# A hybrid decoder layer on one core: w_down and the first gate/up sets with tokens in place

## The chip, the cores and the metric

The kernel runs on one core of a Trainium2 chip. The metric is the device time of one execution in microseconds; lower is better. The median of 3 runs of the kernel before is 2718.86 us, the lowest 2718.18, the highest 2719.04.

## The reference

One layer on 512 tokens of width 2048, all in float32: two token mixers side by side (latent attention and a gated delta rule), then a SwiGLU block. The change touches the end of it:

```
x = x + gt_a * mix
h = rmsnorm(x, norm_ffn) * (1 + sc_f) + sh_f          # (512, 2048)
gate, up = split(h @ w_gate_up)                        # w_gate_up (2048, 2 * 5632)
x = x + gt_f * ((silu(gate) * up) @ w_down)            # w_down    (5632, 2048)
return rmsnorm(x, final_norm)
```

`gt_f` is one vector of 2048 values, from the conditioning vector c.

## The kernel before

**Precision.** Each float32 operand is split into a rounded high half and a rest (`hi`, `lo`; ACT casts, DVE subtracts), and each product is three matmuls into one PSUM bank: high by high, high by low, low by high. In a matmul one operand of 128 x 128 stays in the array (it is loaded by PEld), and the other streams past it, 256 or 512 columns wide. A name like `m<-xh,hi` lists the streaming operand first and the one in place second.

**The order of the work.** Python code makes *units* (`Unit`: load, split, mms, pre, post). `Driver` keeps some units loaded and two split ahead of the one whose matmuls run, and steps side chains between matmuls. All instructions are recorded under one line (`L477`), and `Score` then sets the order on DVE and ACT by a planner: it has a price for each operation (`durations`), a latest start for each (`latest`), and a model of the run (`order`). PE, POOL and SP keep the order of the code. Tiles come from pools: 68 slots of 512 columns, 5 `raws`, 4 `his`, 4 `los`, 8 PSUM banks.

**The SwiGLU block.** `w_gate_up` is worked in 11 sets of 512 gate and 512 up channels (the first two of 256 each). The sets 2 to 11 (`big`) use Strassen's seven products over halves of the tokens and of the inner dimension: 16 units of two sums of weights, their splits and 24 or 18 matmuls of 512 columns, with the tokens in place. Eight PSUM banks hold four products of two token blocks for the first 8 units; three more products are added to them in the other 8. One sum of weights is written to DRAM (`s_dram`) in the first half and read back in the second. The result is turned back to channels by rows with short runs of transposes (`aT`), and kept in DRAM (`f_dram`).

The first two sets are plain. `gu0` runs twice over its weights, once for each half of the tokens, since the second half becomes ready later; `gu_both` works on both halves at once. Both keep the weights in place and stream 256 tokens at a time.

**w_down.** Its 44 blocks of 128 rows are worked as 4 (`dn(36, n)`), 16 in seven-product parts (`strassen_down(0, n)`, n = 0 to 3, 512 channels each), 4 (`dn(40, n)`), 16 in seven-product parts (`strassen_down(1, n)`) and 4 last rows (`last_dn`). A seven-product part has 8 units of 42 matmuls; the weights are in place and 256 tokens stream. Each result is scaled by `gt_ffn` and added in DRAM to `x2_dram`, which holds the residual x, channels by rows: POOL issues a transfer that adds.

**The end.** The residual comes back from `x2_dram` (`back`). For the first 256 tokens `last_unit` keeps the weights in place (`dnl`, 256 columns), and that half of the output leaves channels by rows. For the other 256 the residual is turned (`x2T`, two runs of 16 transposes, copied out by ACT to `x2t`), and `token_unit` keeps the tokens in place (`dnt`, 512 columns); each unit ends with a product with the gate row, a sum, a square with its row sum on ACT, and a product with the row of `final_norm`. After the last unit of a token block, `token_rstd` takes the root in three steps and `scaled` writes the block out. The host puts the two halves together.

Of the kernel before, what the change touches and what calls it, by code (L numbers as in the profile page):

```python
# [144 lines left out]
class Op:  # L145
# [20 lines left out]
    def durations(self):  # L166
# [6 lines left out]
        if self.pe:  # L173
            if self.name == "transpose":
                return 45 + 0.345 * n, 280.0
            if any(a.rounded for a in self.reads):
                return n / 2.4 + 13.5, n / 2.4 + 176.5
            t = 222.0 if n <= 1 else 17.0 if n <= 32 else 116.0 if n <= 64 else n / 0.6 + 9
            return t, t + 165
        if self.engine == "vector":  # L180
            if self.name in ("tensor_tensor", "tensor_copy"):
                d = 148 + 1.05 * n
            elif self.name == "tensor_reduce":
                d = 148 + 1.05 * m
            elif self.name == "reciprocal":
# [96 lines left out]
class Score:  # L282
# [67 lines left out]
    def latest(self):  # L350
# [17 lines left out]
        for _ in range(self.ROUNDS):  # L368
            out, after = [0.0] * n, {}
            for k in range(n - 1, -1, -1):  # L370
                op = ops[k]
                seen = self.LANDING + op.move if op.dma else op.seen
                v = min([out[j] - seen for j in self.users[k] + late[k]], default=end - seen)
                if op.pe:
# [10 lines left out]
    def order(self):  # L385
# [33 lines left out]
        for _ in range(n):  # L419
# [67 lines left out]
def block_kernel(ctx: ExitStack, tc: tile.TileContext, a: dict, out, out_t):  # L487
# [248 lines left out]

    w_in = a["w_in"][0]
# [216 lines left out]
    n_out = C("n_out", [P, 16])  # L954

    def load_scalars():
        load(n_out[:], a["out_norm"])
# [761 lines left out]
    s_ffn, sh_ffn, gt_mix, gt_ffn, gt_neg, gt_mneg = (C(n, [P, 16]) for n in ("s_ffn", "sh_ffn", "gt_mix", "gt_ffn", "gt_neg", "gt_mneg"))  # L1719
# [565 lines left out]
    def strassen_down(ks, n):  # L2285

        def outputs(res):
            for h in range(2):
                for f in range(2):
                    t = res.pop("gp"[f] + str(h))  # L2290
                    for j in range(2):
                        k = 4 * n + 2 * f + j
                        nc.scalar.activation(half_of(t, k), half_of(t, k), AF.Copy, scale=(gt_neg if f else gt_ffn)[:, k:k + 1])
                    nc.gpsimd.dma_start(x2_dram[h, 2 * n + f], t[:], accum_op=ALU.add)
                    yield

        def freed(k):
            if n == 3 and k % 2:
                down[ks][k // 2] = None
                gone[1 + ks] += 1  # L2300

        w = w_dn[2048 * ks:2048 * ks + 2048, :].rearrange("(h k p) n -> k p h n", h=2, p=P)
        return strassen(lambda k: w[k], 512 * n + 256, 512 * n,
                        [(c, i, j, lambda k, c=c: half_k(down[ks][k // 2][c], k)) for c, i, j in PRODUCTS],
                        lambda k: down_ready(ks, k // 2), outputs, freed, still=n == 3)
# [145 lines left out]
    def gu_done(s, ps):  # L2451

        f = {}

        def done(j, h):
            if h == 0:
                return
            for h in range(2):
                fs, v = slice(256 * (j % 2), 256 * (j % 2) + 256), ps[j][:, 256 * h:256 * h + 256]
                if j < 2:  # L2460
                    if j == 0:
                        f[h] = S("sl")
                    nc.scalar.activation(f[h][:, fs], v, AF.Silu)
                else:
                    nc.vector.tensor_tensor(f[h][:, fs], f[h][:, fs], v, ALU.mult)
                if j == 3:
                    side(f_dram[s, h], f[h][:])
        return done

    def gu_both(s):  # L2470

        st = {}

        def unit(k0):
# [8 lines left out]
            def pre():  # L2483
                if k0 == 0:
                    st["ps"] = [PS(f"gu{s}") for _ in range(4)]
                    st["done"] = gu_done(s, st["ps"])

            def after(j, h):
                st["done"](j, h)

            mms = []
            for kk in range(2):
                k = k0 + kk
                for j in range(4):
                    for h in range(2):
                        for n, (wi, xi) in enumerate(((0, 0), (0, 1), (1, 0))):
                            mms.append(lambda kk=kk, k=k, j=j, h=h, n=n, wi=wi, xi=xi: mm(
                                st["ps"][j][:, 256 * h:256 * h + 256], box["w"][wi][:, kk, tok(j)], half_k(h2T[h][k // 2], k)[xi],
                                start=k == 0 and h == 0 and n == 0, stop=k == KT - 1 and n == 2, skip_group_check=True))
                        if k == KT - 1:  # L2500
                            mms[-1] = lambda m=mms[-1], j=j, h=h: (m(), after(j, h))

            def post():
                if k0 + 2 == KT:
                    for q in range(4):
                        h2T[1][q] = None

            return Unit(start, split, mms, pre, post, late=k0 + 2 == KT)
# [3 lines left out]
    def dn_done(n, k0):  # L2512
        def done(ps):
            for j in range(4):
                k = 4 * n + j
                t = S("y")
                nc.scalar.activation(t[:], ps[j][:], AF.Copy, scale=gt_ffn[:, k:k + 1])
                nc.gpsimd.dma_start(x2_dram[:, k // 2, :, 256 * (k % 2):256 * (k % 2) + 256].rearrange("h p n -> p h n"),
                                    t[:].rearrange("p (h n) -> p h n", h=2), accum_op=ALU.add)
# [8 lines left out]
    def ffn():  # L2528
        def gu0():
            us, st = [], {}  # L2530

            def done(ps):
                done_ = gu_done(0, ps)
                for j in range(4):
                    for h in range(2):
                        done_(j, h)

            for h in range(2):
                half = fm_set("gu0", gu_loads(0), 512, KT, lambda k, h=h: half_k(h2T[h][k // 2], k), done if h else None, st=st,
                              cols=slice(256 * h, 256 * h + 256), alone=True)  # L2540
# [5 lines left out]
                us.append(half)  # L2546
# [6 lines left out]
            with_pre(us[0], start)  # L2553
            return us[0] + us[1]
# [6 lines left out]
        def dn(k1, n):  # L2561
            return fm_set(f"dn{k1}_{n}", lambda k0, nk: plain(w_dn, k1 + k0, nk, 512 * n, 512), 512, 4,
                          lambda k: (aT[k1 + k][0][:], aT[k1 + k][1][:]), dn_done(n, k1), late=True)

        LAST = 32
        wl = {}

        def last_weights(n, k0):
# [6 lines left out]
            def split():  # L2575
                raw = box.pop("raw")
                for kk in range(2):
                    wl[n, k0 + kk] = hilo(raw[:, kk, :], "wl")
# [3 lines left out]
        def last_dn():  # L2582

            weights = [last_weights(n, k0) for n in range(4) for k0 in (0, 2)]
            for k, u in enumerate(strassen_down(1, 3)):
                if k == 1:
                    def start():
                        chains["back"] = drv.add(back())
                    with_pre([u], start)
                yield u  # L2590
                for _ in range((0, 0, 0, 0, 0, 0, 1, 1)[k]):
                    yield weights.pop(0)
            for q in range(8):
                u = last_unit(FIRST, [2 * q, 2 * q + 1])
                if q == 0:
                    with_pre([u], lambda: drv.finish(chains["act"]))
                with_pre([u], lambda q=q: back_to(q))
                yield u
                for _ in range(min(2, len(weights))):
                    yield weights.pop(0)  # L2600
            yield act(load_rows)
            yield Unit(pre=lambda: back_to(15), mms=[lambda t=t, n=n: turned(t, n) for t in range(2) for n in range(4)])
            sf = C("sf", [P, 2, 6])
            for t in range(2):
                for n in range(4):
                    for cs in (slice(0, 256), slice(256, 512)) if (t, n) == (1, 3) else (slice(0, 512),):
                        yield token_unit(t, n, sf[:, t, :], cs)

        back_n = [0]

        def back():

            yield from until(lambda: gone[2] >= 1)
            for i in (2, 3):
                reload_a(LAST + i)
                yield
            yield from until(lambda: gone[2] >= 2)
            for h in range(2):
                for q in range(8):
                    if q == 6 and h == 0:  # L2620
# [222 lines left out]
```

## Time and profile before

| | |
|---|---|
| median of 3 runs | 2718.86 us |
| profiled execution | 2718.32 us |
| its span, first to last instruction | 2716.5 us |
| TensorE busy | 2698.4 us, 15304 matmuls |
| VectorE busy | 2130.9 us |
| ScalarE busy | 1213.8 us |
| DMA traffic | 562 MB, 207 GB/s on average |
| mean granted TensorE clock | 0.998 |

PE is TensorE's matmul, PEld its weight load, DVE VectorE, ACT ScalarE, POOL GpSimd, SP SyncE (here it issues loads). Lines of the profile name the output, then the inputs, without buffer numbers. The chain of waits is followed back from the last instruction; it gives the work that nothing else could have been late for.

### The profile page before, as it was taken

Reading aid. Unit: us, or ns where it says so; the run is one execution under the profiler, and the core shown is the slowest. Engines: PE = TensorE matmul, PEld = TensorE weight load, DVE = VectorE, ACT = ScalarE, POOL = GpSimd, SP = SyncE. Lnnn points to the kernel's source line nnn. Section 1 sums busy time; section 2 is a strip of 40 time slices with the busy share of each in tenths; the row PEclk is TensorE's granted clock in tenths of the full one; section 3 lists DMA queues with packets and bytes.
Section 4 is the critical chain, followed back from the end, with each engine's and each line's share of the span. In section 5 each row is a group of like instructions: output and inputs, shape, how many; then the busy total and the mean of one; then the engine's idle time right before and its main releaser. Section 6 shows DMA issues by size and latency. Waiting matters only on the chain.

```text
span 2716.5 us, 41153 instructions
## 1 busy us (share of the span) xinstructions
PE 2698.4 (99%) x15304; PEld 2349.9 (87%) x15304; DVE 2130.9 (78%) x3361; ACT 1213.8 (45%) x1717; POOL 257.7 (9%) x361
## 2 busy tenths in 40 slices
PE   9999999999999999999999999999999999999998
PEld 7888788888888888889999888888888888998997
DVE  8985666776988887688797777778787887878877
ACT  4343432442345343335573444444444446446445
POOL 0000011102001000000000000000000103013113
PEclk9999999999999999999999999999999999999999
DMA  9995555645666889524864566665655669479565
GB/s 352 353 360 195 163 168 170 201 132 178 183 185 210 314 299 325 200 86 125 268 198 143 186 202 202 205 211 200 209 193 192 221 205 224 122 192 209 142 181 173
DMA packets 315490, 562.21 MB, mean 207 GB/s; under 512 B 40772, under 2 KB 120916, under 8 KB 315288
## 3 DMA queue, kind: packets, MB, share of 16 engines
q1 hardware_dynamic: 264776, 458.99, 52.0%
q0 software_dynamic: 31872, 74.76, 10.9%
q10 hardware_dynamic: 18640, 25.83, 2.7%
q8 instruction: 120, 1.97, 0.3%
q14 instruction: 82, 0.67, 0.1%
HBM read 476.62 MB, written 83.89 MB: 206 GB/s over the span
## 4 chain that ended last, share of the span: by engine, by line
PE 99%; issue 0%; DVE 0%; DMA 0%; SPq 0%; ACT 0%; POOLq 0%; DVEq 0%
PE m L477 44%; PE gb L477 6%; PE v L477 4%; PE gu L477 3%; PE z L477 3%; PE ya L477 3%; PE ga L477 3%; PE k L477 3%; PE s L477 3%; PE dn L477 3%; PE q L477 3%; PE yb L477 3%; PE wo L477 2%; PE qk L477 2%; PE cq L477 2%; PE ckv L477 2%
## 5 line engine op out<-in xcount | busy, mean ns | idle before, releaser
L477 ACT CAST hi<-raws 128x1024 fp32r<-128x1024 f32 (+2 forms) x328 | 292.0, 890 | 419.0 <-PE m L477 251.9
L477 ACT CAST hi<-raw 128x1024 fp32r<-128x1024 f32 (+1 forms) x251 | 260.4, 1038 | 473.0 <-DMA raw<-in_w_in_dram 81.5
L477 DVE TENSOR_TENSOR lo<-raws,hi 128x1024 fp32r<-128x1024 f32 (+2 forms) x328 | 332.4, 1022 | 139.8 <-ACT hi L477 137.0
L477 DVE TENSOR_TENSOR lo<-raw,hi 128x1024 fp32r<-128x1024 f32 (+1 forms) x251 | 303.7, 1211 | 166.5 <-ACT hi L477 163.7
L477 PE MATMUL m<-xh,lo 128*128 128x256 f32 x1088 | 307.9, 283 | 0.0
L477 PE MATMUL m<-xl,hi 128*128 128x256 f32 x1088 | 307.9, 283 | 0.0
L477 PE MATMUL m<-xh,hi 128*128 128x256 f32 x1088 | 307.9, 283 | 0.0
L477 ACT CAST hi<-sums 128x1024 fp32r<-128x1024 f32 x168 | 176.4, 1050 | 231.3 <-PE m L477 191.3
L477 DVE TENSOR_TENSOR lo<-sums,hi 128x1024 fp32r<-128x1024 f32 x168 | 205.5, 1223 | 90.4 <-ACT hi L477 88.7
L477 DVE CUSTOM_DVE_ANT_0 rawm<-rawm,cbc 128x1024 f32<-128x1024 f32 x192 | 232.2, 1225 | 19.7 <-DMA rawm<-in_w_mod_dram 19.1
L477 PEld LDWEIGHTS m<-xl,hi 128*128 128x128 f32 x1088 | 208.9, 192 | 0.1
L477 PEld LDWEIGHTS m<-xh,hi 128*128 128x128 f32 x1088 | 208.9, 192 | 0.1
L477 PEld LDWEIGHTS m<-xh,lo 128*128 128x128 f32 x1088 | 208.9, 192 | 0.0
L477 PE MATMUL m<-hi,h2h 128*128 128x512 f32 x480 | 189.9, 396 | 0.0
L477 PE MATMUL m<-hi,h2l 128*128 128x512 f32 x480 | 187.2, 390 | 0.0
L477 PE MATMUL m<-lo,h2h 128*128 128x512 f32 x480 | 187.1, 390 | 0.0
L477 PEld LDWEIGHTS m<-hi,h2l 128*128 128x128 f32 x480 | 90.1, 188 | 18.9
L477 PEld LDWEIGHTS m<-lo,h2h 128*128 128x128 f32 x480 | 90.2, 188 | 17.7
L477 PEld LDWEIGHTS m<-hi,h2h 128*128 128x128 f32 x480 | 90.2, 188 | 17.6
L477 PE MATMUL gb<-hh,hi 128*128 128x512 f32 x256 | 102.0, 398 | 0.0
L477 PE MATMUL gb<-hl,hi 128*128 128x512 f32 x256 | 99.9, 390 | 0.0
L477 PE MATMUL gb<-hh,lo 128*128 128x512 f32 x256 | 99.9, 390 | 0.0
(543 smaller groups left out, 7017.1 us busy)
## 6 DMA issues: line engine op xcount, KB each, us to landing
raws<-in_w_gate_up_dram SPq DMA_DIRECT2D x400, 256.0 KB, 3.7
rawm<-in_w_mod_dram SPq DMA_DIRECT2D x192, 512.0 KB, 5.4
raw<-in_w_in_dram SPq DMA_DIRECT2D x143, 512.0 KB, 4.7
raws<-in_w_down_dram SPq DMA_DIRECT2D x128, 256.0 KB, 3.7
s_dram<-raws POOLq DMA_DIRECT2D x80, 256.0 KB, 3.2
raws<-s_dram SPq DMA_DIRECT2D x80, 256.0 KB, 2.9
rawa<-in_w_in_dram SPq DMA_DIRECT2D x32, 512.0 KB, 4.4
raws<-in_w_o_dram SPq DMA_DIRECT2D x48, 256.0 KB, 2.9
```

What stands on the lines that cost most here:

```text
L477: self.tc.keep_in_program_order(op.call(*op.args, **op.kwargs))
```

## The change

Five things change; the planner's prices change with them.

- *Seven-product parts.* `strassen_down` is replaced by `tokens_down`, the plan of `big` with w_down's weights: tokens in place, 1024 channels a part, 16 units, so 4 parts instead of 8. Weight sums go over `s_dram` and back.
- *Where results are added.* They are now tokens by rows and not scaled; they are added in a new array `down_dram`, `dn(36)` writes it first. The two results of the part before the last stay in SBUF (`kept`), and the last part's go straight into the sums read back.
- *Gate/up's first two sets* (`gu_tokens`) keep the tokens in place and stream 256 gate and 256 up channels together, 512 columns.
- *The last rows.* All 512 tokens are worked with tokens in place. w_down's last rows are multiplied by the gate row before the split. For each block of 128 tokens and 512 channels, x2 is turned straight into the PSUM bank (`turned`), and the 12 products add to it. `finished` adds the sum read back.
- *The end.* One output, tokens by rows. `token_root` needs two DVE instructions a step instead of three, and the last block's last two pieces get root and `final_norm` in one.
- *The planner's prices* for float32 matmuls, memsets, table loads, early transfers and stores.

The core of the diff:

```diff
-            t = 222.0 if n <= 1 else 17.0 if n <= 32 else 116.0 if n <= 64 else n / 0.6 + 9
+            t = 222.0 if n <= 1 else 17.0 if n <= 32 else 116.0 if n <= 64 else max(222.0, n / 1.2 + 29)
...
-                start += 1290.0
+                start = max(start, at[op.engine] + 1290.0)
...
-                done[k] = bus + 640.0 + self.SPARE
+                done[k] = bus + 640.0 + self.SPARE + (1000.0 if 800.0 < start < 6000.0 else 0.0)
...
+    def token_root(ss, inv):
+        v, y, u = (C(nm("rs"), [P, 1]) for _ in range(3))
+        nc.vector.tensor_scalar(v[:], ss, 0.5 * inv, 0.5 * EPS, op0=ALU.mult, op1=ALU.add)
...
+        for _ in range(3):
+            nc.vector.scalar_tensor_tensor(u[:], y[:], v[:, 0:1], y[:], op0=ALU.mult, op1=ALU.mult)
+            nc.vector.scalar_tensor_tensor(y[:], u[:], -1.5, y[:], op0=ALU.add, op1=ALU.mult)
+        return y
...
-    def strassen_down(ks, n):
...
+    def tokens_down(ks, n):
...
+        FIRST4 = [("m1", 0, 1, "m1", part("m1")), ("m6", 0, 0, "m6", part("m6")), ("m7", 1, 0, "m7", part("m7")),
+                  ("m5", 1, 1, "m5", part("m5"))]
+        LAST3 = [("m2", 1, 0, "m1", part("m2")), ("m4", 0, 0, "m7", part("m4")), ("m3", 0, 1, "m5", part("m3"))]
...
+            for c, w, j, bank, x in products:
+                for t in range(2):
+                    for m, (xi, wi) in enumerate(((0, 0), (0, 1), (1, 0))):
+                        def one(c=c, w=w, j=j, bank=bank, x=x, t=t, m=m, xi=xi, wi=wi):
+                            mm(ps[bank][t][:], x(q)[xi][:, 256 * kk + P * t:256 * kk + P * t + P], box["w"][w][wi][:, j, :],
...
+    def add_down(t, n, src, **kw):
+        nc.gpsimd.dma_start(down_dram[t][:, 512 * n:512 * n + 512], src, accum_op=ALU.add)
...
+    def gu_tokens(s, hts):
...
-                                st["ps"][j][:, 256 * h:256 * h + 256], box["w"][wi][:, kk, tok(j)], half_k(h2T[h][k // 2], k)[xi],
+                mm(banks[h, t][:], half_k(h2T[h][k // 2], k)[xi][:, tok(t)], box["w"][wi][:, kk, :],
...
+        def turned(t, n, ps, cs):
...
+                mm(ps[:, P * j - cs.start:P * j - cs.start + P], half_of(x2[h][k // 2], k)[:, tok(t % 2)], ident, is_transpose=True,
+                   start=P * j == cs.start, stop=False, skip_group_check=True)
...
+        def finished(t, n, ps, cs=slice(0, 512)):
+            xt, w, c = s_t[t, n][:, cs], cs.stop - cs.start, n + (cs.start > 0)
+            tmp = S("sq")
+            nc.vector.tensor_tensor(xt, xt, ps[:, 0:w], ALU.add)
+            nc.scalar.activation(tmp[:, 0:w], xt, AF.Square, accum_out=sf[:, t, c:c + 1])
+            if (t, n // 2) != (3, 1):
+                nc.vector.tensor_tensor(xt, xt, rows[4 + n][:, cs], ALU.mult)
...
+                nc.vector.tensor_tensor(raw[:], raw[:], rows[n][:].unsqueeze(1).broadcast_to([P, 2, 512]), ALU.mult)
+                hi, lo = halves(raw, 512, 2)
...
+            def at(i):
+                if i == 2:
+                    back_s(0)
+                elif i == 3:
+                    with_kept(0)
+                    back_s(1)
+                elif i == 4:
+                    with_kept(1)
+                    load_rows(g_dram)
...
+                elif i == 15:
+                    load_rows(a["final_norm"])
```

`back_s` reads four blocks of `down_dram` back into tiles `sd`, `with_kept` adds the kept results, `at(i)` runs ahead of unit i of the last part. In the two programs the matmuls of 512 columns go from 8463 to 10287, those of 256 from 5147 to 1498, and those of 128 from 732 to 780.

On PE, where w_down's last seven-product part ends and its last rows begin (`m`: a product's bank, `dnl` and `dnt`: a bank of the last rows, `x`: the residual, `kc`: the identity), before:

```order
L477 MATMUL m_4260_4400<-xh_4234,hi_4446 128x256
L477 MATMUL m_4260_4400<-xl_4235,hi_4446 128x256
L477 MATMUL m_4260_4400<-xh_4234,lo_4447 128x256
L477 MATMUL dnl_4471<-ah_4297,wlh_4438 128x256
L477 MATMUL dnl_4471<-al_4298,wlh_4438 128x256
L477 MATMUL dnl_4471<-ah_4297,wll_4439 128x256
```

and now:

```order
L482 MATMUL m_4213_4353<-hi_4478,xh_4264 128x512
L482 MATMUL m_4213_4353<-lo_4479,xh_4264 128x512
L482 MATMUL m_4213_4353<-hi_4478,xl_4265 128x512
L482 MATMUL dnt_4490<-kc,x_4277_4417 128x128 x2
L482 MATMUL dnt_4490<-kc,x_4278_4418 128x128 x2
L482 MATMUL dnt_4490<-hi_4484,ah_4453 128x512
L482 MATMUL dnt_4490<-lo_4485,ah_4453 128x512
```

The operands have changed places, the columns have doubled, and four transposes stand ahead of the products of the bank.

On SP, the loads of the last part, where before only weights stood (`raws_4393<-in_w_down_dram 128x2x256` and the like), now (`sd`: a block of the sums so far):

```order
L482 DMA sd_4368<-down_dram 128x512
L482 DMA sd_4369<-down_dram 128x512
L482 DMA sd_4370<-down_dram 128x512
L482 DMA sd_4371<-down_dram 128x512
L482 DMA raws_4377<-in_w_down_dram 128x512
L482 DMA raws_4378<-in_w_down_dram 128x512
L482 DMA raws_4377<-in_w_down_dram 128x512
L482 DMA sd_4379<-down_dram 128x512
```

The weights of a unit wait in the queue behind four blocks that are read back.

On DVE, the end of the program (`rs`: the root's steps, `xo` and `sd`: pieces of the output, `hbc`: the root of the channel-major half), before:

```order
L477 SCALAR_TENSOR_TENSOR rs_4577<-rs_4577,rs_4575 128x1
L477 TENSOR_TENSOR xo_4550<-x2t_4515,row_4513 128x512
L477 TENSOR_TENSOR xo_4556<-x2t_4516,row_4514 128x512
L477 TENSOR_TENSOR xo_4565<-x2t_4517,row_4513 128x512
L477 TENSOR_TENSOR xo_4568<-x2t_4518,row_4514 128x512
L477 SCALAR_TENSOR_TENSOR rs_4576<-rs_4577,rs_4576 128x1
L477 TENSOR_TENSOR xo_4571<-x2t_4518,row_4514 128x256 x2
L477 TENSOR_SCALAR xo_4562<-xo_4562,rs_4576 128x512
L477 TENSOR_TENSOR x_4344_4484<-x_4344_4484,hbc_4549 128x512
```

and now:

```order
L482 SCALAR_TENSOR_TENSOR rs_4556<-rs_4555,rs_4554 128x1
L482 SCALAR_TENSOR_TENSOR rs_4555<-rs_4556,rs_4555 128x1
L482 SCALAR_TENSOR_TENSOR rs_4556<-rs_4555,rs_4554 128x1
L482 SCALAR_TENSOR_TENSOR rs_4555<-rs_4556,rs_4555 128x1
L482 SCALAR_TENSOR_TENSOR sd_4410<-sd_4410,rs_4555,row_4488 128x512
L482 SCALAR_TENSOR_TENSOR sd_4430<-sd_4430,rs_4555,row_4489 128x512
```

Nothing stands between the root's steps any more, and two products follow them instead of ten instructions.

More of the change, by code (lines that the diff above doesn't have):

```diff
@@ L368, in latest @@
         for _ in range(self.ROUNDS):
-            out, after = [0.0] * n, {}
+            out, after, store = [0.0] * n, {}, end
             for k in range(n - 1, -1, -1):
@@ L2449, in gu_loads, with gu_read @@
                                (lambda r: r[:, :, 256:512], wrows(w_gu, k0, nk, DFF + 256 * s, 256))]
[L2451 to L2472, printed above, removed]
+    first_tiles = {}
+    def gu_read(s, ht, bank):
+        if s == 0:
+            first_tiles[ht] = S("g0")
+        o, g = first_tiles[ht][:, 256 * s:256 * s + 256], S("sl")
+        nc.scalar.activation(g[:, 0:256], bank[:, 0:256], AF.Silu)
+        nc.vector.tensor_tensor(o, g[:, 0:256], bank[:, 256:512], ALU.mult)
+    def gu_tokens(s, hts):
+        banks = {}
         def unit(k0):
@@ L2513, in done @@
         def done(ps):
[L2514 to L2519, printed above, removed]
+            for t in range(NT):
+                y = S("y")
+                nc.scalar.copy(y[:], ps[t][:])
+                if k0 == 36:
+                    side(down_dram[t][:, 512 * n:512 * n + 512], y[:])
+                else:
+                    add_down(t, n, y[:])
             plain_sets[0] += 1
@@ new lines, in ffn, with load_rows, back_x, back_s @@
+        sf = C("sf", [P, NT, 6])
+        def load_rows(src):
+            for i in range(4):
+                r = S("row")
+                load(r[:], src[512 * i:512 * i + 512].partition_broadcast(P))
+                rows.append(r)
+        def back_x(n):
+            for h in range(2):
+                for q in (2 * n, 2 * n + 1):
+                    x2[h][q] = S("x2")
+                    side(x2[h][q][:], x2_dram[h, q])
+        def back_s(n):
+            for t in range(NT):
+                s_t[t, n] = S("sd")
+                load(s_t[t, n][:], down_dram[t][:, 512 * n:512 * n + 512])
@@ new lines, in with_kept, with gated @@
+        def with_kept(n):
+            for t in range(NT):
+                h, j = divmod(t, 2)
+                nc.vector.tensor_tensor(s_t[t, n][:], s_t[t, n][:], kept.pop((h, j, n)), ALU.add)
+        def gated(n):
+            for t in range(NT):
+                s_ = s_t[t, n][:]
+                nc.vector.tensor_tensor(s_, s_, rows[n][:], ALU.mult)
+        def turned(t, n, ps, cs):
+            h = t // 2
+            for j in range(cs.start // P, cs.stop // P):
+                k = 4 * n + j
+                mm(ps[:, P * j - cs.start:P * j - cs.start + P], half_of(x2[h][k // 2], k)[:, tok(t % 2)], ident, is_transpose=True,
+                   start=P * j == cs.start, stop=False, skip_group_check=True)
+            if t % 2 and cs.stop == 512:
+                x2[h][2 * n] = x2[h][2 * n + 1] = None
@@ L2576, in split @@
                 raw = box.pop("raw")
+                nc.vector.tensor_tensor(raw[:], raw[:], rows[n][:].unsqueeze(1).broadcast_to([P, 2, 512]), ALU.mult)
+                hi, lo = halves(raw, 512, 2)
                 for kk in range(2):
-                    wl[n, k0 + kk] = hilo(raw[:, kk, :], "wl")
+                    wl[n, k0 + kk] = hi[:, kk, :], lo[:, kk, :]
             return Unit(start, split)
-        def last_dn():
[L2584 to L2589, printed above, removed]
-                yield u
[L2591 to L2620, printed above, removed]
-                        yield from until(lambda: gone[2] == 4 and chains["act"] not in drv.chains)
-                    x2[h][q] = S("x2")
-                    side(x2[h][q][:], x2_dram[h, q])
-                    back_n[0] += 1
-                    yield
@@ L2627, in back_to @@
-        def back_to(n):
-            while back_n[0] <= n:
-                drv.step(chains["back"])
-        FIRST = HALF[:1]
-        rows, x2t = [], []
-        def load_rows():
-            for src in (g_dram, a["final_norm"]):
-                for i in range(2):
-                    raw = raws.tile([P, 2, 512], F32, tag="raw", name=nm("row"))
-                    load(raw[:].rearrange("p j n -> p (j n)"), src[1024 * i:1024 * i + 1024].partition_broadcast(P))
-                    rows.append(raw)
-            for i in range(4):
-                x2t.append(his.tile([P, 2, 512], F32R, tag="hi", name=nm("x2t"))[:].bitcast(F32))
@@ L2745, in ffn @@
         yield from gu0()
-        yield from with_pre(gu_both(1), lambda: xc.append(drv.add(combine())))
+        both = gu_tokens(1, [(h, t) for h in range(2) for t in range(2)])
+        yield from with_pre(both, lambda: xc.append(drv.add(combine())))
         side(g_dram.rearrange("(k p) -> p k", p=P), gt_ffn[:])
-        nc.vector.tensor_scalar(gt_neg[:], gt_ffn[:], -1.0, None, op0=ALU.mult)
         for s in range(1, 11):
@@ L2773, in ffn @@
                 yield with_pre([u], more)[0]
[L2774 to L2778 removed]
+        yield from tokens_down(1, 0)
         yield from last_dn()
```

389 lines of the change are left out of this document (240 added, 149 removed).

## The prediction

> **What bounds the kernel now.** I read the page's busy times, then the chain of waits, then busy time by stage, then single stretches in order of time.
>
> ```profile
> span 2716.5 us, 41153 instructions
> PE 2698.4 (99%) x15304; PEld 2349.9 (87%) x15304; DVE 2130.9 (78%) x3361; ACT 1213.8 (45%) x1717; POOL 257.7 (9%) x361
> ```
>
> TensorE is busy for all but 18 us. That alone does not make it the bound, since a matmul's end is modelled. The chain does; its columns are start, length, what, and how many instructions.
>
> ```profile
> 1386.42 76.31 PE gu L477 x636
> 1604.70 63.96 PE m L477 x282
> 2286.81 161.27 PE m L477 x1344
> 2491.63 161.27 PE m L477 x1344
> 2652.90 23.06 PE dnl L477 x192
> 2706.06 6.47 issue
> ```
>
> Within these pieces one matmul follows another without a gap, so length over count is the price of one: 161.27 / 1344 = 120.0 ns with 256 columns (gu agrees: 76.31 / 636), and 63.96 / 282 = 226.8 ns with 512. Two of 256 cost 240.0 ns. One of 512, the same arithmetic, costs 13.2 ns less. The groups by shape give the widths.
>
> ```profile
> L477 PE MATMUL m<-xh,hi 128*128 128x256 f32 x1088 | 307.9, 283 | 0.0
> L477 PE MATMUL m<-hi,h2h 128*128 128x512 f32 x480 | 189.9, 396 | 0.0
> L477 PE MATMUL gu<-h2h,hi 128*128 128x256 f32 x256 | 72.7, 284 | 0.0
> ```
>
> The mean (283, 396) is the life of one and overlaps its neighbours'; it is not the spacing. The last column, idle before, is zero. By stage (columns: stretch, length, busy of PE, PEld, DVE, ACT, POOL with counts, granted clock, DMA share, GB/s):
>
> ```profile
> 0.00:100.00 100.00, 95.48 (x411) 77.05 (x412) 85.56 (x163) 45.83 (x61) 3.50 (x11) 1.00 0.97 352
> 1369.10:1415.40 46.30, 46.30 (x387) 46.24 (x386) 42.60 (x77) 37.55 (x58) 0.00 (x0) 1.00 0.59 183
> 1604.70:1682.75 78.05, 78.05 (x353) 64.63 (x353) 61.67 (x71) 35.07 (x43) 6.47 (x12) 1.00 0.62 203
> 2286.80:2448.10 161.30, 161.30 (x1346) 161.30 (x1345) 136.22 (x195) 81.11 (x111) 19.45 (x25) 1.00 0.62 164
> 2448.10:2491.60 43.50, 43.50 (x194) 35.99 (x194) 32.39 (x47) 27.90 (x44) 18.30 (x18) 1.00 1.04 220
> 2703.30:2716.50 13.20, 0.00 (x0) 0.00 (x0) 8.09 (x26) 3.48 (x8) 1.45 (x2) 0.68 0.51 186
> ```
>
> So TensorE's instruction stream sets the time, at a granted clock of 1.00, and a tail of 13.2 us follows it. An edit is worth what it takes from that stream or from the tail, less any new wait.
>
> **The change, part by part.** Counts are from the two programs, prices from the rows.
>
> *w_down's seven-product parts.* Before: 8 parts of 336 matmuls of 256 columns, the two 161.27 us pieces, 322.5 us. After: 4 parts of 336 matmuls of 512 columns, each 336 x 0.2268 = 76.2 us, together 304.8. **-17.7 us.** That the new stream can run at 226.8 ns is shown: the gate/up sets already run this very plan (16 units, two sums spilled to DRAM and read back, eight banks held), 78.05 us a set including 16 turns, with PE busy all the time and DVE at 61.67.
>
> *Gate/up's first two sets.* 768 matmuls of 256 (three groups of 256) become 384 of 512: 92.2 - 87.1, **-5.1 us.** The weights still have to be split on DVE, 42.60 us of work in the first set's 46.30; PE will now need about 43.7. Cover is nearly gone; see the stall term.
>
> *The last rows.* 192 dnl matmuls of 256 (23.06 us) become 96 of 512 (21.8): **-1.3 us.** The other half of these rows has 512 columns before and after.
>
> *The turns.* x2 was turned in two runs, 32 transposes; now 64, in 17 short runs each ahead of products in the same bank. Prices: the first pair of rows is a run of four between products, the second pair the old runs from first transpose to first product.
>
> ```profile
> 1673.05 0.60 PE L477 MATMUL aT<-kc,g 128*128 128x128 f32 x4
> 1673.71 0.39 PE L477 MATMUL m<-lo,h2h 128*128 128x512 f32 x1
> 2675.78 1.91 PE L477 MATMUL x2T<-kc,x 128*128 128x128 f32 x16
> 2680.59 0.48 PE L477 MATMUL dnt<-wlh,ah 128*128 128x512 f32 x1
> ```
>
> From 1673.05 to 1673.71 stand four transposes and one product: 0.66 - 0.23 = 0.44 us a run, the slower first product included. 17 x 0.44 = 7.5, less 4.8 (2675.78 to 2680.59, with eight tiny sums in it): **+2.7 us.** The gate/up tiles made with tokens in place need 16 more turns, 4 x 0.44: **+1.8 us.** The copies of turned x2 out of PSUM go; they were ACT's and hidden.
>
> *The tail.* Before, DVE has other work between its last steps.
>
> ```profile
> 2703.30 0.42 DVE L477 TENSOR_TENSOR dn<-dnt,row 128x256 f32<-128x256 f32 x1
> 2704.22 0.42 ACT L477 ACTIVATE dn<-x2t 128x256 f32<-128x256 f32 x1
> 2704.76 0.16 DVE L477 TENSOR_REDUCE sf<-sf 128x1 f32<-128x5 f32 x1
> 2705.52 0.35 DVE L477 SCALAR_TENSOR_TENSOR rs<-rs,rs 128x1 f32<-128x1 f32 x2
> 2705.91 0.16 DVE L477 TENSOR_TENSOR rs<-rs 128x1 f32<-128x1 f32 x1
> 2706.76 2.49 DVE L477 TENSOR_TENSOR xo<-x2t,row 128x512 f32<-128x512 f32 x4
> 2712.56 0.72 POOL L477 DMA_DIRECT2D out_dram<-x  x1 [6.50 <-issue]
> ```
>
> Four row products (2.49), and after them the scaling of the channel-major half, stand in the old tail; the new order has neither. New tail from PE's end: add 0.46, square to reduce 0.54, reduce and two scalar steps 0.6, six root steps at 0.195 (two in 0.39) 1.2, two products of 512 at most 1.5 beside ACT's two: 4.3 us to the last issue. From the last issue (2712.56) to the span's end are 3.9. 8.2 instead of 13.2: **-5.0 us**, between -3 (one more 2.5 us group slips in) and -6.
>
> *The start.* The planner's new costs let ACT make the first tokens' high half ahead of a cast.
>
> ```profile
> 9.57 0.83 ACT L477 CAST hi<-raw 128x768 fp32r<-128x768 f32 x1
> 10.31 0.72 ACT L477 ACTIVATE hh<-xT,s_mix 128x512 fp32r<-128x512 f32 x1
> ```
>
> That is 0.74 us earlier at best, nothing if the next loads bind; **-0.4 us.** Reordered small steps further on lie under a full TensorE: zero, and as much as a few tenths each if a wait came in.
>
> *New stalls.* None is in the trace, so bounds. Last part (336 products, 76.2 us): DVE gets 31 instructions of 1024 columns and 54 of 512; last rows (some 51 us of PE): 13 and 42, and 36 tiny ones.
>
> ```profile
> L477 DVE TENSOR_TENSOR lo<-raws,hi 128x1024 fp32r<-128x1024 f32 x160 | 195.9, 1224 | 114.8 <-ACT hi L477 112.6
> L477 DVE TENSOR_TENSOR euvw<-euvw,m 128x512 f32<-128x512 f32 x113 | 73.6, 684 | 1.3
> ```
>
> 31 x 1.224 + 54 x 0.684 = 74.9, and 15.9 + 28.7 + 36 x 0.16 = 50.4; together 125 of PE's 127 us. Back to back they are cheaper (four of 512 in 2.49, 0.62 each), so about 115 in truth. From nothing to 8.8 us (125 at the 92% that DVE reached, 42.60 / 46.30, is 136). I take **+2.5**, most of it here and some 0.5 in gate/up's first set, nearer to nothing, because that 92% was reached without a wait on PE.
>
> Sum: -17.7 - 5.1 - 1.3 + 2.7 + 1.8 - 5.0 - 0.4 + 2.5 = -22.5 us. The profiled execution took 2718.32 (span 2716.5 and 1.8 around it), 0.5 under the median of 2718.86; from the median, 2696.4.
>
> One rule speaks against the main term. The Trainium skill ("TensorE: Matmul & The Clock Gate", Back-to-back issue gap) spaces warm matmuls at N / 2.4 + 2.5 ns, so a halved count would save 2.6 ns a pair, an estimate of 4.7 us for 1824 pairs, and the sum would be about -3. The rows have 120.0 and 226.8, some 13 ns above N / 2.4 at both widths, and the measurement decides.
>
> **The rivals.**
>
> *DVE becomes the bound at the end.* For: 125 of 127 us by its durations; it has new sums with kept parts, gate products and row products there. Against: the overlap just told, and up to two units of products, some 10 us, lie split ahead. At 92% it is 2696.4 + 8.8 - 2.5 = 2703; at the 84% of the old w_down stretch (136.22 / 161.30) 125 becomes 149, 22 over, 2716. By the cheaper price (115 of 127) it costs time once DVE cannot hold 90%.
>
> *Slower: transfers bind the last part.* There 72 blocks of 256 KB stand on SP's queue (the sums so far, rows and weights) and 30 on POOL's: 26.7 MB in 76.2 us, 351 GB/s. DMA then paces sums, splits and products.
>
> ```profile
> raws<-in_w_down_dram SPq DMA_DIRECT2D x128, 256.0 KB, 3.7
> x_dram<-y POOLq DMA_DIRECT2D x32, 256.0 KB, 7.7
> 11.87 87.26 PE s L477 x383
> ```
>
> For: in the stage with added transfers the engines were full (1.04) at 220 GB/s. At that rate the part takes 121 us, 45 over; 10 are swallowed by the units ahead: 2696.4 - 2.5 + 35 = 2729. Against: that stage's x_dram transfers add in DRAM and land in 7.7 us; none of the 102 does, and plain loads ran at 352 GB/s in the first 100 us, while from 11.87 on PE took 383 products at 228 ns. It is slower than before where the rate falls below 26.7 MB / (76.2 + 10 + 25) = 240 GB/s.
>
> *The count doesn't matter.* If the 256-column products are slow for their stage's sake (PEld is busy for 161.30 of 161.30 there) and the new ones meet the same limit, they come at 2 x 120.0 = 240 ns, and the three first terms, 24.1 us, are lost: 2720.5. Against: PEld has a rest wherever 512 columns run (64.63 of 78.05), and 226.8 ns holds there. The rule of the Trainium skill's TensorE page above would end near this one, at an estimate of 2716.
>
> **How the numbers follow.** Forecast 0.77 (its own range 2693 to 2702: stall 0 to 6 and tail -6 to -3 move it by -3.5 to +5.5), DVE 0.14, transfers 0.06, count 0.03. What a measurement can tell from no change is 0.2%, 5.4 us. Faster: 0.77 and nearly all of DVE, 0.89. Same: the count and DVE's far end, 0.05. Slower: 0.06. The range leaves out transfers, count and DVE's upper part: 2690.5 (another 2 us for the start and a cheaper pace of the turns) to 2708.
>
> **What would show it.** Right: pieces of 336 products of 512 columns in the chain at 76 us, no idle PE in the w_down stretch, last product to end near 8 us, DVE over 90% in the last 127 us with PE idle under 4. Wrong: spacing above 0.23, PE idle behind lo (DVE) or behind DMA in the last part, a tail above 10 us.

## The result, and the profile after

The changed kernel takes 2733.3 us (median of 4; 2731.6 to 2734.2) against 2718.95: a ratio of 1.0053, 95% interval 1.0035 to 1.0070. It was forecast at 2696.4 and is slower than before. The profiled execution took 2731.62, span 2729.8, 13.3 more than before's 2716.5.

The page's first part, the two costliest groups of the w_down products and the group of weight sums:

```profile
span 2729.8 us, 37437 instructions
PE 2695.4 (99%) x13518; PEld 2263.3 (83%) x13518; DVE 2124.8 (78%) x3257; ACT 1181.6 (43%) x1648; POOL 230.1 (8%) x363
...
L482 PE MATMUL m<-lo,xh 128*128 128x512 f32 x448 | 178.6, 399 | 9.2 <-DVE lo L482 8.9
L482 PE MATMUL m<-hi,xh 128*128 128x512 f32 x448 | 177.6, 396 | 9.3 <-ACT hi L482 9.3
L482 DVE TENSOR_TENSOR sums<-raws,raws 128x1024 f32<-128x1024 f32 x112 | 136.5, 1219 | 26.2 <-DMA s_dram<-raws 23.8
```

"99% busy" now hides waits: before, the last column was 0.0 for the products; here it has 9.2 and 9.3 us, in front of w_down's products, and DVE's sums waited 23.8 us for stores of `s_dram` to land. The chain of waits is no longer one of matmuls (its longest pieces from 2500 us on):

```profile
2496.16 8.11 issue
2506.44 8.70 DMA s_dram<-raws
2538.68 64.01 PE m L482 x281
2602.87 8.21 DMA raws<-in_w_down_dram
2617.02 14.58 DMA raws<-in_w_down_dram
2631.66 13.47 DMA sd<-down_dram
2669.58 51.22 PE dnt L482 x268
```

64.01 / 281 is 227.8 ns: the products have the pace that was forecast (226.8). What stands between them wasn't there before. Busy time of the four parts in order (stretch, length, PE, PEld, DVE, ACT, POOL, granted clock, mean busy share of the 16 transfer engines, which can pass 1 in the profile's count, GB/s), and of 40 us inside the last:

```profile
2290.60:2366.70 76.10, 76.10 (x337) 63.04 (x336) 67.46 (x82) 38.95 (x50) 5.68 (x11) 1.00 0.66 216
2366.70:2451.70 85.00, 79.96 (x337) 65.08 (x337) 58.38 (x67) 35.17 (x43) 16.41 (x24) 0.96 0.83 248
2495.30:2582.10 86.80, 78.89 (x337) 64.16 (x336) 63.77 (x75) 35.74 (x45) 9.59 (x14) 0.96 0.69 200
2582.10:2669.40 87.30, 81.77 (x337) 62.93 (x336) 69.61 (x86) 28.76 (x32) 16.06 (x30) 0.98 0.85 303
2610.00:2650.00 40.00, 36.26 (x146) 27.56 (x145) 27.20 (x37) 12.09 (x16) 13.36 (x25) 0.96 1.04 386
```

The first part takes 76.1 us, where 76.2 were forecast, with TensorE busy throughout. The other three, of the same 336 products, take 85.0, 86.8 and 87.3: 30.8 us are lost.

Where the 13.3 us come from, by the same marks in the timelines of the two traces: a stage ends at the start of the next stage's first product, or, for `yb`, gate/up's first sets and the two `dn`, at the start of its own last product.

| stage | before | after | difference | forecast |
|---|---|---|---|---|
| to the end of `s` | 98.96 | 100.02 | +1.1 | -0.4 |
| to the end of `yb` | 1101.57 | 1101.85 | +0.3 | 0 |
| attention's and w_o's products up to gate/up | 168.56 | 173.89 | +5.3 | 0 |
| gate/up, first two sets | 93.35 | 88.66 | -4.7 | -5.1, and some 0.5 of stalls |
| gate/up, the other sets, and `dn(36)` | 823.97 | 825.95 | +2.0 | +1.8 |
| w_down, first two of the four new parts | 161.50 | 161.39 | -0.1 | -8.9 |
| `dn(40)` | 43.32 | 43.29 | 0 | 0 |
| w_down, other two | 161.50 | 174.38 | +12.9 | -8.9, and some 2 of stalls |
| last rows | 50.25 | 51.09 | +0.8 | +1.4 |
| from the last product's start | 13.57 | 9.33 | -4.2 | -5.0 |

### The profile page after: what moved, and what is told of

It is laid out like the page before. It is cut to its first block, busy times and chain, and to the rows that moved or that the text cites. A ratio compares the mean times of both kernels' runs of the same rounds, so it can differ in the third digit from the quotient of the medians.

```text
span 2729.8 us, 37437 instructions
## 1 busy us (share of the span) xinstructions
PE 2695.4 (99%) x13518; PEld 2263.3 (83%) x13518; DVE 2124.8 (78%) x3257; ACT 1181.6 (43%) x1648; POOL 230.1 (8%) x363
## 5 line engine op out<-in xcount | busy, mean ns | idle before, releaser
L482 ACT CAST hi<-raw 128x1024 fp32r<-128x1024 f32 (+2 forms) x259 | 268.5, 1038 | 475.3 <-DMA raw<-in_w_in_dram 79.4
L482 DVE TENSOR_TENSOR lo<-raw,hi 128x1024 fp32r<-128x1024 f32 (+2 forms) x259 | 313.1, 1210 | 170.4 <-ACT hi L482 168.5
L482 DVE TENSOR_TENSOR lo<-sums,hi 128x1024 fp32r<-128x1024 f32 x136 | 166.1, 1222 | 47.2 <-ACT hi L482 46.9
L482 PE MATMUL m<-lo,xh 128*128 128x512 f32 x448 | 178.6, 399 | 9.2 <-DVE lo L482 8.9
L482 PE MATMUL m<-hi,xh 128*128 128x512 f32 x448 | 177.6, 396 | 9.3 <-ACT hi L482 9.3
L482 PE MATMUL m<-hi,xl 128*128 128x512 f32 x448 | 176.8, 395 | 0.0
L482 DVE TENSOR_TENSOR sums<-raws,raws 128x1024 f32<-128x1024 f32 x112 | 136.5, 1219 | 26.2 <-DMA s_dram<-raws 23.8
L482 POOL DMA_DIRECT2D s_dram<-raws x112 | 64.1, 578 | 690.5 <-DVE raws L482 680.6
L482 PEld LDWEIGHTS m<-lo,xh 128*128 128x128 f32 x448 | 85.6, 191 | 33.2 <-DVE lo L482 15.6
L482 PEld LDWEIGHTS m<-hi,xh 128*128 128x128 f32 x448 | 85.5, 191 | 29.5 <-ACT hi L482 11.6
L482 PEld LDWEIGHTS m<-hi,h2l 128*128 128x128 f32 x480 | 90.1, 188 | 18.9
```

The lines of the kernel that those rows point to most:

```text
L482: self.tc.keep_in_program_order(op.call(*op.args, **op.kwargs))
```

## The experiments

Three places had lost time, each with a suspect of its own: w_o's stage, the second and third part, the last part. Each kernel below ran for 3 rounds against the kernel before on its chip (the last one 5).

**What stops the second and third part.** The timeline at the longest stall, POOL, DVE and PE (start, length, instruction, in brackets the idle time ahead of it and what ended it):

```profile
2494.38 0.88 POOL L482 DMA_DIRECT2D down_dram<-g  x1 [3.65 <-DMA down_dram<-y]
...
2504.28 3.48 POOL L482 DMA_DIRECT2D down_dram<-y  x4 [8.12 <-issue]
2506.44 1.89 POOL L482 DMA_DIRECT2D s_dram<-raws  x1
...
2515.22 1.22 DVE L482 TENSOR_TENSOR sums<-raws,raws 128x1024 f32<-128x1024 f32 x1 [11.95 <-DMA s_dram<-raws]
...
2518.43 0.79 PE L482 MATMUL m<-hi,xh 128*128 128x512 f32 x1 [6.68 <-ACT hi L482]
```

POOL waits for one adding transfer to land before it issues the next to the same block, 3.65 and then 8.12 us. (For the second wait the profile names no cause, but the semaphore that counts the landing of the adding transfer issued at 2494.95 had its last update at 2503.78.) The store of weight sums stands behind them, leaves at 2506.44 and lands 8.70 us later. It reads a tile of the five `raws`; DVE's next sums need that slot and come at 2515.22; ACT's cast and PE follow.

*The stores on another queue.*

```diff
-                side(s_dram[n % 2, k], r[:, 0, :])
+                nc.scalar.dma_start(s_dram[n % 2, k], r[:, 0, :])
```

> The changed kernel, with the 32 stores of weight sums of the seven-product parts (`s_dram`) issued by ACT instead of POOL; nothing else is edited. Theory, POOL's queue: there these stores stand behind transfers that add to `down_dram`, each of which waits for the one before it on the same block; a store that leaves late holds a `raws` slot, DVE's next sums wait for the slot and PE for DVE. Then the stalls in units 4 to 6 of the second part (4.6 us) and 2 to 6 of the third (10.7 us) go and those of the last part (about 11 us) stay: some 15 us less, 2716 to 2721. Rival, full transfer engines: the stores land as late from any queue, and the time stays within 3 us of 2733.

2711.4 us (ratio to before 0.9971, 0.9959 to 0.9982): 21.9 less than the changed kernel. That is more than expected: a stall of 4.2 us in unit 10 of the second part went too, and 2 of the last part's 11. Its chain of waits and its last two parts:

```profile
2290.84 152.60 PE m L482 x672
2443.44 43.52 PE dn L482 x192
2486.96 76.17 PE m L482 x336
```

```profile
2486.80:2563.00 76.20, 76.20 (x338) 63.10 (x337) 62.80 (x75) 36.05 (x45) 6.13 (x7) 1.00 0.76 219
2563.00:2648.20 85.20, 80.42 (x338) 64.58 (x336) 71.40 (x89) 29.51 (x33) 12.89 (x24) 0.96 0.89 318
```

The first two parts are one piece of 672 products at 227 ns, the third is full as well: the adds, the bytes and DVE's work are the same, only the queue is another. The last part keeps 9 us. The rival, full transfer engines, falls for these parts.

*The adds as plain writes, the order left as it was.*

```diff
-        nc.gpsimd.dma_start(down_dram[t][:, 512 * n:512 * n + 512], src, accum_op=ALU.add)
+        nc.gpsimd.dma_start(down_dram[t][:, 512 * n:512 * n + 512], src)
```

> The changed kernel, with the transfers to `down_dram` writing instead of adding, so the sums over w_down's four pieces are left out; order and waits are the same. Theory, POOL's queue: what the stores of weight sums stand behind are landings of adding transfers, 6 to 11 us each one after the other; plain writes land in about half of that, so the 15 us of stalls in the second and third part fall to 8 or less, 2726 or less. Rival, the order alone: with the same chain of waits the stalls stay, 2731 to 2734. Both leave the last part's 11 us.

2714.4 us (0.9981, 0.9971 to 0.9990), 18.9 less; the first pair of parts takes 152.55 us, the third 76.7, and the last keeps its stalls (88.5). The `down_dram` transfers up to 2560 us, first in the changed kernel and then here (instruction, count, ns of issue on POOL, starts; then landing):

```profile
L482 POOL DMA_DIRECT2D down_dram<-y x22: 540/859/1865, 2279.7 to 2505.9; - x22
...
DMA to landing us min/median/max: 2.7/7.7/14.3
```

```profile
L482 POOL DMA_DIRECT2D down_dram<-y x24: 540/540/540, 2279.8 to 2491.7; - x24
...
DMA to landing us min/median/max: 2.6/5.3/8.2
```

So it takes both: adds that land slowly (7.7 us against 5.3 in the median, and a longer issue) and a store queued behind them that holds a weight slot. Either alone costs next to nothing in these two parts: nothing with the stores on ACT, 0.5 us in the third part with the plain writes.

**What stops w_o.** One instruction stands in that stretch that stood elsewhere before: POOL's store of the gate row, 8 KB, by its access pattern in 2048 pieces of 4 bytes. The timeline of POOL, before and after:

```profile
1420.01 1.21 POOL L477 DMA_DIRECT2D f_dram<-sl  x2 [115.93 <-DVE sl L477]
1421.21 1.18 POOL L477 DMA_DIRECT2D g_dram<-gt_ffn  x1
```

```profile
1300.75 4.66 POOL L482 DMA_DIRECT2D x<-x_dram  x8
1305.40 1.18 POOL L482 DMA_DIRECT2D g_dram<-gt_ffn  x1
```

The code asks for it at the same place. Before, it stood behind two stores that waited 115.93 us for set 0's result; the tokens-in-place set has no such stores, and the row leaves 116 us earlier, while w_o's weights are loaded. The 9 us from 1311 on, before and after:

```profile
1311.00:1320.00 9.00, 9.00 (x77) 9.00 (x76) 4.28 (x5) 4.71 (x6) 0.00 (x0) 1.00 1.08 363
```

```profile
1311.00:1320.00 9.00, 9.00 (x77) 9.00 (x76) 3.41 (x3) 2.14 (x3) 0.00 (x0) 1.00 1.16 99
```

The engines are as busy (1.16) but move 99 GB/s instead of 363, and weights come late. TensorE waits 0.53 us for DVE's `lo` ahead of 1338.61 and then for the squares of the residual (`hss`), a wait that the kernel before doesn't have:

```profile
1354.14 1.05 PE L482 MATMUL hss<-ones,sq 128*128 128x1 f32 x8 [2.35 <-DVE sq L482]
```

From 1355.7 to 1359.2 the granted clock is 0.51.

*The store moved away from there.*

```diff
-        side(g_dram.rearrange("(k p) -> p k", p=P), gt_ffn[:])
...
+                if (s, i) == (1, 4):
+                    with_pre([u], lambda: side(g_dram.rearrange("(k p) -> p k", p=P), gt_ffn[:]))
```

> The changed kernel, with one instruction moved: the 8 KB store of the gate row (`g_dram<-gt_ffn`, 2048 pieces of 4 bytes) is issued by POOL during the second gate/up set's successor (unit 4 of set 2 of the big ones' first) instead of at 1305 us. Theory, small pieces: it slowed all transfers to 60 to 100 GB/s for 9 us, w_o's weights came late, and PE lost 5.3 us between 1337 and 1369 us; without it 2728. Rival, the planner's new order of DVE is what made w_o late: the order there is the same in this kernel, so nothing changes, 2733.

2730.0 us. w_o's stage fell from 173.89 to 168.57, before's value, and its 9 us moved 366 GB/s; but the other gate/up sets rose from 825.95 to 828.64, with a wait of 2.39 us ahead of 1506.6. There too the store met loads that were needed: it was issued at 1482.2, the engines moved 57 and 25 GB/s in the two stretches of 4 us from 1486 on, and DVE waited 4.30 us for gate/up weights until 1498.67. Half the gain was given back.

*The same store early in the kernel before.*

```diff
+        side(g_dram.rearrange("(k p) -> p k", p=P), gt_ffn[:])
         yield from gu0()
...
-        side(g_dram.rearrange("(k p) -> p k", p=P), gt_ffn[:])
```

> The kernel before, with one instruction moved: POOL issues the gate row's store (8 KB in pieces of 4 bytes) right behind the eight `x<-x_dram` loads, at about 1304 us, where the changed kernel has it, and not at 1421 us behind the two `f_dram<-sl` stores. Theory, small pieces: the stretch of w_o from 1322 to 1369 us grows by the 5.3 us that the changed kernel lost there; 2719 becomes 2724. Rival, it was something else of the change: 2719.

2724.7 us against 2718.7 (ratio 1.0022, 1.0013 to 1.0031). This stage alone changed, from 168.56 to 174.47, at 86 GB/s:

```profile
1311.00:1320.00 9.00, 9.00 (x77) 9.00 (x76) 2.77 (x3) 2.09 (x2) 0.00 (x0) 1.00 0.97 86
```

Its chain of waits leads from w_o's weights to the wait at `hss`:

```profile
1311.34 16.14 DMA raw<-in_w_o_dram
...
1337.95 4.57 DMA raw<-in_w_o_dram
```

One moved instruction, in a kernel without the rest of the change, makes the whole loss of that stage. That it is the size of the pieces is not shown: no run stores the row in larger ones.

**What stops the last part.** In its 40 us from 2610 the transfer engines ran at a share of 1.04 and 386 GB/s without a pause, while DVE was busy for 27.20.

*Eight blocks of x2 asked for later.*

```diff
-                elif i == 13:
-                    back_x(2)
-                elif i == 14:
-                    back_x(3)
...
+                        if (n, k0) in ((0, 2), (1, 0)) and t == 1:
+                            u = begin(lambda n=n: back_x(2 + n))(u)
```

> The changed kernel, with the last 8 blocks of x2 that come back (`x<-x_dram`, 256 KB each) asked for during the last rows instead of in units 13 and 14 of the last part. Theory, transfers bind the last part: its stalls of 11 us lie where the engines run at 387 GB/s without a pause from 2610 to 2650 us; 2.1 MB less is 5.4 us, so some 5 to 6 us less, 2727 to 2729. Rival, DVE binds it: the same operations stand on DVE, and the time stays at 2733 (within 2).

2727.5 us, 5.8 less. In the profiled execution (2724.68, the fastest of its 8) 4.0 lie in the second pair of parts (174.38 to 170.43). The first pair lost 2.7 less too, which the edit doesn't explain; the kernel with the moved gate store had that as well (158.63), so such stalls vary by that much from run to run. Nor did the edit do what it was meant to: all eight blocks still left during the last part, six of them between 2626 and 2632 and two at 2644.8, since POOL issued them as soon as tiles came free, and the part moved 26.5 MB as it had before (26.4). So this run is no test of fewer bytes; it only shows that a small shift of these loads is worth some 4 us.

**The planner's prices put back.**

```diff
-            t = 222.0 if n <= 1 else 17.0 if n <= 32 else 116.0 if n <= 64 else max(222.0, n / 1.2 + 29)
+            t = 222.0 if n <= 1 else 17.0 if n <= 32 else 116.0 if n <= 64 else n / 0.6 + 9
...
-                start = max(start, at[op.engine] + 1290.0)
+                start += 1290.0
...
-                done[k] = bus + 640.0 + self.SPARE + (1000.0 if 800.0 < start < 6000.0 else 0.0)
+                done[k] = bus + 640.0 + self.SPARE
```

> The changed kernel with the planner's prices of before (but for the transposes). Theory: the new prices have to do with the start alone, where PE lost 1.1 us against before up to 100 us; 2732, with the w_down stalls as they were. Rival, the order that the new prices give DVE and ACT makes the stalls in the w_down parts: 2710 or less.

2732.4 us, 0.9 less, with the same stalls (161.14 and 176.45 in the two pairs). The order that the new prices give DVE and ACT isn't the cause of these stalls.

**Together.** Three edits: ACT's queue, eight late blocks, and the gate row tied to set 0's end so that it leaves at 1427 us:

```diff
+        if s == 0 and ht == (1, 1):
+            r = C("gt_row", [P, 16])
+            nc.vector.scalar_tensor_tensor(r[:], o[:, 0:16], 0.0, gt_ffn[:], op0=ALU.mult, op1=ALU.add)
+            side(g_dram.rearrange("(k p) -> p k", p=P), r[:])
...
-        side(g_dram.rearrange("(k p) -> p k", p=P), gt_ffn[:])
```

> The changed kernel with three edits: the stores of weight sums on ACT's queue; the last 8 blocks of x2 asked for in the last rows; the gate row's store tied to the end of set 0 (one more small DVE instruction makes POOL wait for it), so that it leaves at about 1420 us as before. If the three causes are separate, the gains add up: -22 and -5.8 measured and -5.3 from the trace give 2700 (2697 to 2703). Rival, they share a cause (transfers): a good deal less, 2706 or more.

2703.65 us, just above the upper end: the gains nearly add up. The last pair of parts still took 158.96, where the first without stalls takes 152.6.

> As the one with three edits, but 12 blocks of x2 are asked for in the last rows and not 8. In the kernel with ACT's stores alone the last part still lost 9 us, at 387 GB/s without a pause; 3.1 MB less is 8.1 us. Theory, transfers bind the last part: 1 to 3 us below the one with three edits. Rival, DVE binds it (125 us of work by its durations in 127 us): no further gain, or some tenths lost where the blocks come too late for their turns.

The diff is the same with `back_x(1)` moved too. 2701.6 us: 2.0 less, within what transfers were expected to give. But in the traces the last part gained only 0.65 of that (81.48 to 80.83), and the third part 1.1, so this run does not decide between the two. One more edit to this kernel puts the twelve late blocks on SP's queue:

```diff
-                    side(x2[h][q][:], x2_dram[h, q])
+                    (load if n else side)(x2[h][q][:], x2_dram[h, q])
```

> As the kernel with three edits and 12 late blocks of x2, but SP issues these 12 and not POOL. On POOL's queue nothing held them: they left between 2597 and 2618 us, as soon as tiles came free, in the stretch where the engines moved 380 to 390 GB/s; on SP's they stand behind the last part's weights. Theory, transfers: the last part's remaining 4.6 us of stalls fall to 1 to 3, 2698.5 to 2700.5 against 2701.6. Rival, DVE: no gain (2701 to 2702.5). Third way: SP's queue now holds the last rows' weights behind these blocks, and the last rows lose what the last part gains.

2697.5 us (ratio to before 0.9927, 0.9914 to 0.9941), a little under what was expected; the last rows lost nothing (51.17 for 51.09). It beats both kernels. Its last two parts, and all that PE waited for DVE there in the table of waits:

```profile
2481.10:2557.20 76.10, 76.10 (x337) 63.02 (x336) 63.14 (x75) 36.12 (x45) 6.13 (x7) 1.00 0.75 218
2557.20:2634.60 77.40, 76.93 (x338) 62.79 (x337) 69.83 (x85) 29.24 (x33) 6.50 (x12) 1.00 0.95 339
```

```profile
PE m L482 <- DVE lo L482: 0.5, 1, 0.5
```

The last part takes 77.4 us at 339 GB/s, and DVE, 90% busy, does not stop it. The bytes are nearly the same, 26.3 MB; their order is another. The twelve blocks now leave between 2620 and 2630, behind the last part's weights, and in this part a read of weight sums lands in 5.9 us in the median, where it took 9.2 in the changed kernel and 8.4 in the kernel before this one.

## Why the prediction was wrong

**The step that failed is "New stalls".** It asked one question, whether DVE has time enough, and took +2.5 us out of 0 to 8.8. The stalls cost 30.8 in w_down, and DVE's load made almost none of them: with the three causes gone the last two parts lose 1.2 us, and TensorE waits 0.5 us for DVE, at 90%. The size of DVE's load was right: 114.94 us of work in the last part and the last rows, where about 115 was estimated.

- *The queue wasn't costed.* The term w_down rested on the gate/up sets, which run the same plan without a stall. That proof held for PE's pace and for DVE, not for POOL: in gate/up no adding transfers stand ahead of the stores of weight sums, in w_down they do. The change put 32 urgent stores into a queue that in w_down had held, before, adds that no engine waited for, and loads of the last rows. 18.9 to 21.9 us, by two independent edits.
- *"Reordered small steps ... lie under a full TensorE: zero."* One of these steps was the gate row's store, which the change freed from its cover: two stores taken out ahead of it. 5.3 us, shown in both directions. A full TensorE hid the instruction, but not the loads that its transfer slowed.
- *The transfers rival had the right place and the wrong form.* It set 351 GB/s of need against 220 GB/s of supply, saw 45 us or nothing, and gave it 0.06. The supply was there (386 GB/s in 40 us of the changed kernel, 339 over the whole part in the last one). The loads were bunched: the blocks read back late in the part fell together with the weights of units 10 to 15. 11 us of the loss were there. 2 of them went with the stores on ACT's queue; of the other 9, ordering the same bytes anew took all but 1.2 away. That this rival's 2729 lies near the 2733.3 is luck: it put 35 us there.
- *The other rivals.* DVE as the bound at the end: refuted as above. The count doesn't matter: refuted, 76.17 / 336 is 226.7 ns against 240.

**The other terms held.** w_down's parts take 76.1 us each where nothing stops them; gate/up's first sets gave -4.7 (-4.6 forecast, with 0.5 of stalls); the turns of `aT` +2.0 (+1.8); last rows +0.8 (+1.4), with the run price right:

```profile
2669.42 0.60 PE L482 MATMUL dnt<-kc,x 128*128 128x128 f32 x4
2669.77 0.48 PE L482 MATMUL dnt<-hi,ah 128*128 128x512 f32 x1
2670.09 0.39 PE L482 MATMUL dnt<-lo,ah 128*128 128x512 f32 x1
```

From 2669.42 to 2670.09 are 0.67, less 0.23: 0.44. The tail gave 4.2 of 5.0:

```profile
2720.83 0.42 DVE L482 TENSOR_TENSOR sd<-sd,dnt 128x256 f32<-128x256 f32 x1 [0.56 <-PE dnt L482]
...
2722.39 1.31 DVE L482 SCALAR_TENSOR_TENSOR rs<-rs,rs 128x1 f32<-128x1 f32 x6
...
2725.10 0.84 ACTq L482 DMA_DIRECT2D out_dram<-sd  x2
```

DVE's steps took nearly what was forecast. The estimate of 4.3 us from PE's end at 2720.8 to the last issue fits the first of the last two stores (2725.10); the last one began at 2725.53, 4.7 us after PE's end, and from there to the span's end it was 4.3 and not 3.9. The start went the other way: +1.1, not -0.4. The first product came 0.06 us earlier, and then PE waited 1.1 us for DVE's `hl`; with the prices put back the first product came at 11.76 instead of 11.02, yet `s` ended 0.4 earlier. Over all these kernels the stretch varies from 98.9 to 100.1, so its cause stays open.

The sum without the stalls was therefore near: 2697.5 us is what the same change takes when its transfers are placed so that almost nothing waits. That it is only 1.1 above the forecast is in part luck, since the forecast holds 2.5 us of stalls. Without them the sum is 2693.9, and the 3.6 above it are 1.2 of stalls left in the last two parts, 1.0 that the tail did not give, and some 0.7 each in gate/up's other sets and up to the end of `yb`, with smaller differences both ways.

## What to carry to other kernels

A plan that runs without a stall in one stage proves its engines there, not its queues: list for each queue what stands ahead of the moved transfers in the new stage, and who holds a slot until they land. An in-order queue shouldn't mix stores on which a buffer waits with adds to DRAM that wait for each other. And when something is taken out of a queue, ask what it was holding back: the next transfer then leaves early, and may land in the busiest stretch.

## What the hardware showed that wasn't expected

A stall costs more than itself. After the gap of 6.68 us the products from 2520.28 to 2522.84 came 0.43 us apart, and only those from 2523.20 on at 0.23 again (PE, start and life):

```profile
2518.43 0.79 PE L482 MATMUL m<-hi,xh 128*128 128x512 f32 x1 [6.68 <-ACT hi L482]
2519.69 0.80 PE L482 MATMUL m<-lo,xh 128*128 128x512 f32 x1 [0.47 <-DVE lo L482]
2520.28 0.63 PE L482 MATMUL m<-hi,xl 128*128 128x512 f32 x1
2520.71 0.63 PE L482 MATMUL m<-hi,xh 128*128 128x512 f32 x1
...
2523.20 0.39 PE L482 MATMUL m<-hi,xh 128*128 128x512 f32 x1
2523.42 0.39 PE L482 MATMUL m<-lo,xh 128*128 128x512 f32 x1
```

From 2518.4 to 2526.6 the granted clock was 0.71. In w_down some 25 products came 0.2 us late in this way, 5 us on top of the waits; that is a part of why 18 us of waits became 30.8. The Trainium skill ("TensorE: Matmul & The Clock Gate", Part 1, on the clock gate) states that after an idle window of about 3.4 us the array runs at half clock, 426.7 ns for 512 columns, until some 3.4 us of work. The trace agrees for the pace. For the gap it differs: the same slow pace followed idle times of 1.95, 2.32 and 2.46 us too, and the measurement decides.

An 8 KB store in 4-byte pieces held the transfers of the whole core at 86 to 99 GB/s for some 9 us, where 363 ran without it. The Trainium skill ("DMA: Bandwidth & Descriptors", Specifications) asks for pieces of at least 512 bytes for the full rate. The runs fit this, though none stores the row in larger pieces, and they show that the transfers beside the store pay as well.
